# The opening of a hybrid decoder block: chunk-wise start, and conditioning rounds split evenly between DVE and PE

## The chip, the cores and the metric

One core of a Trainium2 chip runs the kernel. The metric is the device time of one execution in microseconds (us). PE is the matrix engine and PEld its weight load, DVE the vector engine, ACT the scalar engine, POOL the general one; SP only issues transfers. Each engine works through its own instructions in order and waits for others by semaphores.

## The reference

One layer of a decoder block, 512 positions, 2048 channels, all float32. What matters here is its first part; the rest (projections, a gated linear recurrence, windowed attention, branch merge, output projection, MLP) is unchanged.

```
ada = silu(c) @ w_ada + b_ada          # 2048 -> 6 x 2048
shift1, scale1, gate1, shift2, scale2, gate2 = split(ada, 6)
h = rms_norm(x, norm1_g) * (1 + scale1) + shift1
proj = h @ w_in                        # then 11 parts of proj
```

## The kernel before

Everything is kept transposed: channels lie on the 128 partitions, the 512 positions along the row. So x and h are 16 chunks of 128x512, and every weight is cut into 128x128 pieces. For accuracy each product of a weight with h is three products in fp32r (`mm3`): the weight and h are each split into a rounded part and the rest (`hi`, `lo`), and hi*hi, hi*lo and lo*hi are added up. ACT makes `hi` (L160), DVE makes `lo` (L127).

The weights arrive in raw loads of 512 KB (three buffers, tag `raw`), each of which is two items of 128x512. `step()` handles one item: `pump_loads()` issues on SP every raw load that is allowed, at most three ahead of the split that is due; `pump_splits()` splits items up to two ahead of the one at hand; `pump_loads()` is called again; then the item's products are issued. A raw load into a buffer waits until the items of the load that was in it have been split.

`startup()` makes h and drives the first eight loops. Loop j multiplies the two h chunks 2j and 2j+1 with the weights of 12 output tiles: six steps of 12 products each. Four output tiles stay in PSUM over all loops, the other eight are added up in SBUF (`sums`, tag `O`) by DVE after each loop's products. While loop j runs, the shift and scale of the next two chunks are made, the conditioning: a vector-matrix product over 16 K-tiles of `wada1`, 256 KB each, tag `O`. They are taken in four rounds of four K-tiles: in `ada_round` the first NDV K-tiles are multiplied and accumulated by DVE (`ada_step`, tile `aa`), the others by PE, four at a time in four groups of 32 columns. At the end of a round `prefetch(KT * j + 4 * r + 4 + NADA)` asks SP for the tiles up to 12 beyond the round. `ada_end` sums over the partitions on PE (columns), and `make_h` scales, shifts and splits the two chunks. `SCH` says after which of the six steps each round comes: round 0 after step 0, round 1 after step 1, rounds 2 and 3 after step 2, `ada_end` and `make_h` after step 3. With NDV = 4, round 0 is DVE's.

All bulk transfers, x, conditioning tiles and raw loads, are issued by SP in the order in which the program reaches them. Small constants are loaded by POOL at the start. Before loop 0, x is squared and summed for the norm, and the conditioning of chunks 0 and 1 is made from 16 tiles, all on PE.

Of the kernel before, what the change touches and what calls it, by code (L numbers as in the profile page):

```python
# [10 lines left out]
F32 = mybir.dt.float32  # L11
# [6 lines left out]
P = 128  # L18
# [14 lines left out]
FIRST = ("ident", "adaT")  # L33
FILL = 288
SKEW = (1, 3)
NDV = 4
SCH = ((0,), (1,), (2, 3), (4, 5), (), ())
BUFS = {"A": 32, "O": 25, "C": 16, "T": 6, "L": 5, "ada": 3, "raw": 3, "wt": 4, "B": 32, "S": 2}
WT = 7 * 2 * P
MLP = ("B", "S")  # L40
# [49 lines left out]


@with_exitstack
def tile_block(ctx, tc, xT, cT, wada1, wada2, badaT, g1T, g2T, wg0, win, wbat, wbhg, wout, wfg, wst,
               wff2, lbT, hggT, qgT, kgT, sinks, table, ident_d, mask_d, onehot_d, neg_d, outT):
    nc = tc.nc
    pl = Plan()
# [18 lines left out]
    def nm(s):  # L115
        uid[0] += 1
        return f"{s}_{uid[0]}"
# [54 lines left out]
    def take(tag, shape=None, dt=F32, name=None):  # L172
        pl.live[tag] = pl.live.get(tag, 0) + 1
        return home(tag).tile(shape or [P, T], dt, tag=tag, bufs=BUFS[tag], name=nm(name or tag))
# [12 lines left out]
    def mx():  # L187
        pl.live["mx"] = pl.live.get("mx", 0) + 1
        return psM.tile([P, T], F32, tag="mx", name=nm("mx"))
# [5 lines left out]
        return tiny.tile([P, n], F32, tag="s", bufs=8, name=nm("s"))  # L195


    def cload(name, shape, src, dt=F32):
        t = (fst if name in FIRST else cst).tile(shape, dt, name=name)
        G.dma_start(out=t, in_=src)  # L200
        return t

    c_sb = cload("c_sb", [P, KT], cT)
    x_t = []
    for kt in range(KT):
        t = take("C")
        SP.dma_start(out=t, in_=xT[:, kt, :])  # L207
        x_t.append(t)
    g1_sb = cload("g1_sb", [P, KT], g1T)
    adaT = cload("adaT", [P, 96], badaT)  # L210
    tab_sb = cload("tab_sb", [32, 16], table)
    oneh = take("T", [32, 383])
    G.dma_start(out=oneh, in_=onehot_d)
    negc = take("T", [16, 383])
    G.dma_start(out=negc, in_=neg_d)
    ident = cload("ident", [P, P], ident_d)
    qg_sb = cload("qg_sb", [P, 1], qgT)
    kg_sb = cload("kg_sb", [P, 1], kgT)
# [117 lines left out]
    raws = {}  # L336
    wts = {}

    def pump_loads():
        done = items[state["split"]][0] if state["split"] < len(items) else len(loads)  # L340
        while state["load"] < len(loads) and state["load"] < done + BUFS["raw"]:
            src, n = loads[state["load"]]
            if state["load"] in doubled and not room("S") and not room("T", 5):
                return
            raw = act.tile([P, n], F32, tag="raw", bufs=BUFS["raw"], name=nm("raw"))
            if state["load"] in doubled:
                n -= 2 * P
                raw = raw[:, 0:n]
                full, src = src, src[:, 0:n]
            SP.dma_start(out=raw, in_=src)  # L350
            if state["load"] in doubled:
                c = 2 * P
                tag = "S" if room("S") else "T"
                s = take(tag)
                SP.dma_start(out=s, in_=src[:, 0:2 * c])
                G.dma_start(out=s.rearrange("p (n c) -> p n c", c=c),  # L356
                            in_=full[:, None, 3 * c:4 * c].to_broadcast([P, 2, c]), accum_op=ALU.add)
                raw = (raw, s, tag)
            raws[state["load"]] = raw
            state["load"] += 1  # L360
# [129 lines left out]
                drop("O")  # L490

    held = {}
    for j in range(KT // 2):
        for g in range(G0 // 2):
            if g % 2 == 0:
                ld = add_load(wg0[j, g // 2], 1024)

            def emit(hi, lo, j=j, g=g):
                for s in range(2):
                    i = 2 * g + s  # L500
                    if i not in HELD:
                        ps = mx()
                    elif j == 0:
                        ps = held[i] = acc() if i in HELD[:NACC] else mx()
                    else:
                        ps = held[i]
                    stop = i not in HELD or j == KT // 2 - 1
                    for k in range(2):
                        c = slice((2 * s + k) * P, (2 * s + k + 1) * P)
                        mm3(ps, hi[:, c], lo[:, c], h[2 * j + k], (i not in HELD or j == 0) and k == 0, stop and k == 1)  # L510
                    start_evac(i, j, ps)
            add_item(ld, (g % 2) * T, T, emit)
    n_start = len(items)

# [99 lines left out]
    def xload(n):  # L614
        def pre():
            xr[n] = take("T")
            SP.dma_start(out=xr[n], in_=xT[:, n, :])
        return pre

    def out_post(n):  # L620
# [450 lines left out]
    rv = dram.tile([16, 383], F32, name="rv")  # L1071
    rap = rv[:, :]

    def bias_rows():
        psb = mx()
        mm(psb[0:16, 0:383], tab_sb, oneh)
        tt(negc, psb[0:16, 0:383], negc, ALU.add)
        drop("mx")
        G.dma_start(out=rv, in_=negc)
        drop("T", 2)  # L1080

    def startup():
        nf = [0]
        raw = {}

        def prefetch(n):
# [3 lines left out]
                SP.dma_start(out=raw[j, kt], in_=wada1[j, kt])  # L1090
                nf[0] += 1

        prefetch(NADA)
        ps = mx()
        for kt in range(KT):
            sq = take("T")
            sact(sq, x_t[kt], AF.Square)
            if kt % 2 == 0:
                sq0 = sq
            else:  # L1100
                tt(sq, sq0, sq, ALU.add)
                mm(ps, ones, sq, kt == 1, kt == KT - 1)
                drop("T", 2)
        c32 = take("L", [P, KT, 32])
        vcopy(c32, c_act[:, :, None].to_broadcast([P, KT, 32]))
        r1, w = take("T"), take("T")
        run(rstd_g(ps, 1.0 / D, r1, w))
        drop("T")
        drop("mx")
        for kt in range(2):  # L1110
            tt(x_t[kt], x_t[kt], r1, ALU.mult)
        make_lb()
        cell = {}

        def ada_round(j, r):
            nd = NDV if j else 0
            if r == 0:
                cell["ps"] = mx()
                if nd:
                    cell["a"] = ada_acc()  # L1120
            ps = cell["ps"]
            for g in range(4):
                kt = 4 * r + g
                if kt < nd:
                    ada_step(cell["a"], raw.pop((j, kt)), kt)
                else:
                    mm(ps[32 * g:32 * g + 32, :], c32[:, kt, :], raw.pop((j, kt)), 4 * r == nd, r == 3)
                drop("O")
            prefetch(KT * j + 4 * r + 4 + NADA)
            if r == 3:  # L1130
                cell["s"] = take("L")
                if nd:
                    stt(cell["s"], ps, sel, cell["a"], ALU.mult, ALU.add)
                else:
                    sact(cell["s"], ps, AF.Copy)
                drop("mx")

        def ada_end(j):
            cell["ps"] = mx()
            ada_cols(cell["s"], cell["ps"], one if NDV and j else sel)  # L1140
            drop("L")

        def make_h(j):
            c0 = 2 * j
            ps = cell["ps"]
            tt(adaT[:, 16 + c0:18 + c0], ps[:, 2:4], adaT[:, 16 + c0:18 + c0], ALU.add)
            tt(adaT[:, c0:c0 + 2], ps[:, 0:2], adaT[:, c0:c0 + 2], ALU.add)
            drop("mx")
            stt(G1[:, c0:c0 + 2], adaT[:, 16 + c0:18 + c0], 1.0, g1_sb[:, c0:c0 + 2], ALU.add, ALU.mult)
            for kt in (c0, c0 + 1):  # L1150
                t, s, b = x_t[kt], G1[:, kt:kt + 1], adaT[:, kt:kt + 1]
                hi, lo = take("A", dt=F32R), take("A", dt=F32R)
                if j == 0:
                    sact(hi, t, AF.Identity, scale=s, bias=b)
                    ts(t, t, s, ALU.mult, b, ALU.add)
                    tt(lo, t, hi.bitcast(F32), ALU.subtract)
                else:
                    stt(t, t, s, r1, ALU.mult, ALU.mult)
                    sact(hi, t, AF.Identity, bias=b)
                    stt(lo, t, b, hi.bitcast(F32), ALU.add, ALU.subtract)  # L1160
                drop("C")
                h.append((hi, lo))

        for r in range(4):
            ada_round(0, r)
            if r == 0:
                pump_loads()
            if r == 2:
                bias_rows()
        pump_splits(1)  # L1170
        ada_end(0)
        make_h(0)
        for j in range(8):
            if j == 6:
                mask_load()
            for g in range(G0 // 2):
                step(2, drive=False)
                if j < 7:
                    for r in SCH[g]:
                        if r < 4:  # L1180
                            ada_round(j + 1, r)
                        elif r == 4:
                            ada_end(j + 1)
                        else:
                            make_h(j + 1)
# [467 lines left out]
```

## Time and profile before

| | |
|---|---|
| median of 3 runs | 2715.68 us (2715.46 to 2717.07) |
| the profiled execution | 2714.99 us, its span 2713.2 us |
| busy in the span | PE 2694.4, PEld 2288.8, DVE 1681.7, ACT 1037.3, POOL 153.3 us |
| first product of a weight with h | 31.80 us after the span's start |
| loops 1 to 6 | 20.62 us each on PE |

Busy time says what an engine did, not what bounded it; that is read from the chain of work that ended last and from timelines. In a timeline row, the first number is the start and the second the time to the end of the group; a value in brackets is the idle time of that engine ahead of it, with what ended it. Rows of one engine can overlap at their ends, so times from start to start are used for sums.

### The profile page before, as it was taken

The page shows a single profiled execution, that of the slowest core. Times are in us where ns is not written, and L with a number is a line of the kernel's source. Part 1 is how long each engine was busy: PE and PEld are TensorE (multiplying, and loading weights), DVE is VectorE, ACT ScalarE, POOL GpSimd, SP SyncE. Part 2 cuts the span into 40 slices and gives each one's busy share as a digit, 9 for nine tenths or more (in the row PEclk, how much of TensorE's full clock was granted, in tenths as well). Part 3 has the DMA queues.
Part 4 walks back from the last instruction along what each step waited for, and adds up shares of the span by engine and source line. Part 5 has one row for each costly group of instructions (what it writes and reads, how often), then busy time and mean ns, then how long its engine had stood idle before and what let it go on. Part 6 is the DMA issues. An engine that isn't in the chain of part 4 may idle for free.

```text
span 2713.2 us, 38663 instructions
## 1 busy us (share of the span) xinstructions
PE 2694.4 (99%) x14742; PEld 2288.8 (84%) x14742; DVE 1681.7 (62%) x3223; ACT 1037.3 (38%) x1905; POOL 153.3 (6%) x144
## 2 busy tenths in 40 slices
PE   8999999999999999999999999999999999999999
PEld 4777777888888888888888899988999888999897
DVE  4778777655444545565387666666566655666664
ACT  4245355544222322232254334333344333433341
POOL 1000000000000000000001011110011100111110
PEclk9999999999999999999999999999999999999999
DMA  8852321344555565555334445654455544555453
GB/s 328 291 188 97 121 97 67 121 152 132 192 190 189 182 198 175 189 168 203 129 107 127 127 131 145 156 139 126 128 144 148 148 129 127 141 146 150 131 139 127
DMA packets 182649, 415.49 MB, mean 153 GB/s; under 512 B 18944, under 2 KB 48768, under 8 KB 182464
## 3 DMA queue, kind: packets, MB, share of 16 engines
q1 hardware_dynamic: 149760, 380.18, 42.9%
q0 software_dynamic: 32704, 32.85, 7.8%
q8 instruction: 116, 1.90, 0.3%
q14 instruction: 69, 0.57, 0.1%
HBM read 408.72 MB, written 4.23 MB: 152 GB/s over the span
## 4 chain that ended last, share of the span: by engine, by line
PE 98%; DVE 1%; DMA 0%; ACT 0%; issue 0%; SPq 0%; ACTq 0%
PE acc L164 70%; PE mx L164 27%; PE mx L168 1%; DMA C<-xT 0%; DVE L L131 0%; DVE wt L127 0%; DVE T L127 0%; DVE s L1267 0%; DVE C L131 0%; DVE C L138 0%; DVE s L127 0%; SPq L207 0%; ACT T L160 0%; ACT wt L160 0%; ACT L151 0%
## 5 line engine op out<-in xcount | busy, mean ns | idle before, releaser
L164 PE MATMUL acc<-A,wt 128*128 128x512 f32 (+1 forms) x5160 | 1138.0, 368 | 4.1 <-ACT A L160 1.9
L164 PEld LDWEIGHTS acc<-A,wt 128*128 128x128 f32 x5160 | 910.7, 189 | 174.1 <-issue 8.6
L160 ACT ACTIVATE wt<-raw 128x512 fp32r<-128x512 f32 (+1 forms) x820 | 528.8, 662 | 867.2 <-PE acc L164 605.2
L127 DVE TENSOR_TENSOR wt<-raw,wt 128x512 fp32r<-128x512 f32 (+1 forms) x820 | 594.8, 729 | 422.6 <-ACT wt L160 421.1
L164 PE MATMUL acc<-B,wt 128*128 128x512 f32 (+1 forms) x3540 | 734.0, 359 | 0.0
L164 PEld LDWEIGHTS acc<-B,wt 128*128 128x128 f32 x3540 | 612.3, 189 | 98.6
L164 PE MATMUL mx<-A,wt 128*128 128x256 f32 (+1 forms) x2448 | 425.5, 309 | 0.0
L164 PEld LDWEIGHTS mx<-A,wt 128*128 128x128 f32 x2448 | 359.4, 191 | 29.5 <-issue 5.0
L164 PE MATMUL mx<-B,wt 128*128 128x256 f32 (+1 forms) x1620 | 293.9, 319 | 0.0
L131 DVE SCALAR_TENSOR_TENSOR C<-acc,adaT,C 128x512 f32<-128x512 f32 x211 | 158.0, 749 | 206.4 <-PE acc L164 206.4
L164 PEld LDWEIGHTS mx<-B,wt 128*128 128x128 f32 x1620 | 247.4, 191 | 20.3
L356 POOL DMA_DIRECT2D S<-wst x87 | 104.0, 1196 | 2065.7 <-ACT B L160 1155.2
L423 DVE SCALAR_TENSOR_TENSOR ada<-ada,aa 128x512 f32<-128x512 f32 x256 | 175.3, 685 | 47.4 <-DMA ada<-wada 42.4
L164 PE MATMUL acc<-O,wt 128*128 128x512 f32 x768 | 178.6, 389 | 0.0
L164 PEld LDWEIGHTS acc<-O,wt 128*128 128x128 f32 x768 | 144.2, 188 | 29.9
L160 ACT ACTIVATE T<-T 128x256 f32<-128x256 f32 (+1 forms) x218 | 104.4, 508 | 109.4 <-DVE T L127 106.8
L160 ACT ACTIVATE wt<-T 128x512 fp32r<-128x512 f32 x145 | 87.8, 621 | 76.7 <-DVE T L127 74.5
L127 DVE TENSOR_TENSOR wt<-T,wt 128x512 fp32r<-128x512 f32 x145 | 96.8, 684 | 0.0
L127 DVE TENSOR_TENSOR T<-T,raw 128x256 f32<-128x256 f32 x145 | 61.5, 424 | 28.1 <-DMA T<-wst 24.1
L160 ACT ACTIVATE T<-acc 128x512 f32<-128x512 f32 x34 | 20.3, 597 | 152.6 <-PE acc L164 152.6
L127 DVE TENSOR_TENSOR T<-S,raw 128x256 f32<-128x256 f32 x87 | 36.7, 421 | 42.7 <-DMA S<-wst 38.6
L160 ACT ACTIVATE B<-T 128x512 fp32r<-128x512 f32 x80 | 47.3, 602 | 34.0 <-DVE T L127 19.8
(170 smaller groups left out, 1350.1 us busy)
## 6 DMA issues: line engine op xcount, KB each, us to landing
raw<-win SPq DMA_DIRECT2D x128, 512.0 KB, 4.0
ada<-wada SPq DMA_DIRECT2D x256, 256.0 KB, 4.4
raw<-wff SPq DMA_DIRECT2D x128, 512.0 KB, 3.6
raw<-wst SPq DMA_DIRECT2D x116, 384.0 KB, 3.7
O<-wada SPq DMA_DIRECT2D x128, 256.0 KB, 5.2
S<-wst SPq DMA_DIRECT2D x87, 256.0 KB, 3.9
S<-wst POOLq DMA_DIRECT2D x87, 256.0 KB, 4.3
raw<-wout SPq DMA_DIRECT2D x32, 512.0 KB, 4.0
```

What stands on the lines that cost most here:

```text
L127: nc.vector.tensor_tensor(out=out, in0=in0, in1=in1, op=op)
L131: nc.vector.scalar_tensor_tensor(out=out, in0=in0, scalar=scalar, in1=in1, op0=op0, op1=op1)
L160: nc.scalar.activation(out=out, in_=in_, func=func, **kw)
L164: PE.matmul(out, lhsT=lhsT, rhs=rhs, start=start, stop=stop)
L168: PE.transpose(out=out, in_=in_, identity=ident)
L356: G.dma_start(out=s.rearrange("p (n c) -> p n c", c=c), in_=full[:, None, 3 * c:4 * c].to_broadcast([P, 2, c]), accum_op=ALU.add)
L423: nc.vector.scalar_tensor_tensor(out=t, in0=t, scalar=1.0, in1=cb, op0=ALU.mult, op1=ALU.mult, accum_out=adaq[:, i, q:q + 1])
```

## The change

- The weights of the conditioning of chunks 0 and 1 come a second time as `wada0`, 16 tiles of 256 KB, of which the first eight hold all that chunk 0 needs and the other eight all that chunk 1 needs. `first_chunk(s)` makes one chunk from eight tiles. Chunk 0 is made before loop 0, chunk 1 within step 1 of loop 0.
- In loop 0, items 0 to 2 are first multiplied with chunk 0 alone, and with chunk 1 when it is there. Small products on constants (`keep`) run on PE between the pieces of the first chunk.
- SP's order at the start: 16 tiles of x, six of `wada0`, a raw load, two of `wada0`, a raw load, eight of `wada0`, a raw load, eight tiles of the next pair. x lies in memory as 16 contiguous blocks.
- Ten small loads move from POOL at the start to SP ahead of loop 1; the bias product (`bias_rows`) and `make_lb` move from the opening to the start of loop 2. Four of the 16 squares of x go to DVE.
- NDV becomes 8: rounds 0 and 1 are DVE's. `ada_rounds` is a generator that stops after the third and the sixth K-tile, so DVE's eight K-tiles come as three after step 0, three after step 1 and two after step 2, where rounds 2 and 3 on PE follow. In loop 0 (`SCH0`) six come after step 2, the others with rounds 2 and 3 after step 3, and `ada_end` and `make_h` after step 4.
- `make_h` makes both scaled chunks and both rounded parts before the two rests.

```diff
-NDV = 4
-SCH = ((0,), (1,), (2, 3), (4, 5), (), ())
+NDV = 8
+SCH0 = ((), (), (0, 1), (2,), (4, 5), ())
+SCH = ((0,), (1,), (2,), (4, 5), (), ())
...
-        SP.dma_start(out=t, in_=xT[:, kt, :])
+        SP.dma_start(out=t, in_=xT[kt])
...
+            def two_products(i, k):
+                todo2 = []
+                for i, ps, w in begun[i:i + 2]:
+                    c = slice((2 * (i % 2) + k) * P, (2 * (i % 2) + k + 1) * P)
+                    mm(ps, w[0][:, c], h[k][0], k == 0, False)
+                    mm(ps, w[1][:, c], h[k][0], False, False)
+                    todo2.append((ps, w[0][:, c], i not in HELD and k == 1))
+                for ps, wc, last in todo2:
+                    mm(ps, wc, h[k][1], False, last)
...
+                if j == 0 and g < 3:
+                    for i in (2 * g, 2 * g + 1):
+                        begun.append((i, bank(i, j), (hi, lo)))
+                    two_products(2 * g, 0)
+                    if g == 1:
+                        second.pop()()
+                    if g < 2:
+                        return
+                    for i in range(0, 6, 2):
+                        two_products(i, 1)
+                        for i, ps, _ in begun[i:i + 2]:
+                            start_evac(i, j, ps)
+                    return
...
+    def load_rest():
+        for t, src in late_loads:
+            SP.dma_start(out=t, in_=src)
...
-        prefetch(NADA)
+        fetch0(KT // 2 - 2)
+        pump_loads(1)
+        fetch0(KT // 2)
+        pump_loads(2)
+        fetch0(KT)
+        pump_loads()
+        prefetch(KT + 8)
...
         def ada_round(j, r):
-            nd = NDV if j else 0
+            nd = NDV
...
                 if kt < nd:
                     ada_step(cell["a"], raw.pop((j, kt)), kt)
+                    if g == 2 and r == 0 or g == 1 and r == 1:
+                        yield
                 else:
                     mm(ps[32 * g:32 * g + 32, :], c32[:, kt, :], raw.pop((j, kt)), 4 * r == nd, r == 3)
                 drop("O")
             prefetch(KT * j + 4 * r + 4 + NADA)
...
+        def ada_rounds(j):
+            for r in range(4):
+                yield from ada_round(j, r)
...
+        def first_chunk(s):
+            x, g, b = x_t[s], G1[:, s:s + 1], adaT[:, s:s + 1]
+            if s == 0:
+                tt(x, x, r1, ALU.mult)
+                pump_splits(0)
+            ps = mx()
+            for i in range(KT // 2):
+                for u in range(2):
+                    kt, t = 2 * i + u, raw0[KT // 2 * s + i]
+                    mm(ps[32 * (kt % 4):32 * (kt % 4) + 32, 0:256], c32[:, kt, :], t[:, 256 * u:256 * u + 256], kt < 4,
+                       kt > KT - 5)
+                drop("O")
+                if s == 0 and i % 2:
+                    keep(1)
...
+            if s == 0:
+                keep(7)
...
         for j in range(8):
+            if j == 1:
+                rest = load_rest()
+            if j == 2:
+                make_lb()
+                bias_rows(*rest)
...
                 step(2, drive=False)
                 if j < 7:
-                    for r in SCH[g]:
+                    for r in (SCH if j else SCH0)[g]:
                         if r < 4:
-                            ada_round(j + 1, r)
+                            if r == 0:
+                                cell["go"] = ada_rounds(j + 1)
+                            next(cell["go"], None)
```

## Rows read from the trace of the kernel before

**Rows 1.** The page: chain of work that ended last, share by engine.
```profile
PE 98%; DVE 1%; DMA 0%; ACT 0%; issue 0%; SPq 0%; ACTq 0%
```

**Rows 2.** Timeline of PE, loop 1: start, us, engine, line, operation, out<-in, count.
```profile
55.22 1.52 PE L164 MATMUL acc<-A,wt 128*128 128x512 f32 x6
...
57.94 1.52 PE L164 MATMUL acc<-A,wt 128*128 128x512 f32 x6
...
63.25 1.52 PE L164 MATMUL mx<-A,wt 128*128 128x512 f32 x6
64.70 1.92 PE L164 MATMUL mx<-O,L 128*32 128x512 f32 x16
66.56 3.06 PE L164 MATMUL mx<-A,wt 128*128 128x512 f32 x12
...
75.84 0.39 PE L164 MATMUL acc<-A,wt 128*128 128x512 f32 x1
```

**Rows 3.** Timeline of SP's issues, 39 to 66 us, two of them singly.
```profile
39.38 0.33 SPq L350 DMA_DIRECT2D raw<-wg  x1
...
56.20 0.33 SPq L350 DMA_DIRECT2D raw<-wg  x1
56.62 1.81 SPq L1090 DMA_DIRECT2D O<-wada  x4
58.05 0.38 SPq L1090 DMA_DIRECT2D O<-wada  x1
62.22 0.33 SPq L350 DMA_DIRECT2D raw<-wg  x1
...
64.78 0.43 SPq L1090 DMA_DIRECT2D O<-wada  x1
```

**Rows 4.** DMA issues at 0.74, 39.38, 58.05, 64.78: KB, us from issue to landing.
```profile
C<-xT SPq DMA_DIRECT2D x1, 256.0 KB, 2.7
raw<-wg SPq DMA_DIRECT2D x1, 512.0 KB, 5.1
O<-wada SPq DMA_DIRECT2D x1, 256.0 KB, 4.5
O<-wada SPq DMA_DIRECT2D x1, 256.0 KB, 4.9
```

**Rows 5.** Timeline of DVE in loop 1, 58 to 62 us.
```profile
58.14 0.69 DVE L127 TENSOR_TENSOR O<-mx,O 128x512 f32<-128x512 f32 x1 [0.48 <-PE mx L164]
58.75 0.48 DVE L136 TENSOR_SCALAR aa<-O,c_act 128x512 f32<-128x512 f32 x1
59.27 2.33 DVE L131 SCALAR_TENSOR_TENSOR aa<-O,c_act,aa 128x512 f32<-128x512 f32 x3
61.51 0.68 DVE L127 TENSOR_TENSOR wt<-raw,wt 128x512 fp32r<-128x512 f32 x1
```

**Rows 6.** Timeline of PE and its weight load, 25 to 32 us.
```profile
25.51 0.81 PE L164 MATMUL mx<-T,tab_sb 32*16 32x383 f32 x2
26.25 1.91 PE L164 MATMUL mx<-O,L 128*32 128x512 f32 x8
27.11 0.14 PEld L164 LDWEIGHTS mx<-O,L 128*32 128x32 f32 x2 [0.49 <-DMA O<-wada]
31.80 0.49 PE L164 MATMUL acc<-A,wt 128*128 128x512 f32 x1 [1.91 <-ACT A L160]
```

**Rows 7.** The chain's first pieces: start, us, what; the second is x's 14th tile.
```profile
0.74 0.39 SPq L207
...
8.92 6.60 DMA C<-xT
```

**Rows 8.** One loop: stretch, length, busy us (count) by engine, PEclk, DMA share, GB/s.
```profile
104.65:125.27 20.62, 20.62 (x105) 14.82 (x105) 15.34 (x27) 4.90 (x8) 0.00 (x0) 1.00 0.80 280
```

**Rows 9.** The same columns for two stretches of the opening.
```profile
20.00:30.00 10.00, 9.21 (x38) 2.63 (x34) 5.38 (x16) 3.19 (x7) 0.51 (x1) 1.00 1.04 411
30.00:40.00 10.00, 7.38 (x24) 5.57 (x24) 7.24 (x15) 3.16 (x5) 0.00 (x0) 0.83 1.05 408
```

More of the change, by code (lines that the diff above doesn't have):

```diff
@@ L92, in tile_block @@
 @with_exitstack
-def tile_block(ctx, tc, xT, cT, wada1, wada2, badaT, g1T, g2T, wg0, win, wbat, wbhg, wout, wfg, wst,
+def tile_block(ctx, tc, xT, cT, wada0, wada1, wada2, badaT, g1T, g2T, wg0, win, wbat, wbhg, wout, wfg, wst,
                wff2, lbT, hggT, qgT, kgT, sinks, table, ident_d, mask_d, onehot_d, neg_d, outT):
@@ L195, in small, with cload @@
         return tiny.tile([P, n], F32, tag="s", bufs=8, name=nm("s"))
-    def cload(name, shape, src, dt=F32):
-        t = (fst if name in FIRST else cst).tile(shape, dt, name=name)
-        G.dma_start(out=t, in_=src)
+    late_loads = []
+    def cload(name, shape, src, now=False):
+        t = (fst if name in FIRST else cst).tile(shape, F32, name=name)
+        if now:
+            G.dma_start(out=t, in_=src)
+        else:
+            late_loads.append((t, src))
         return t
-    c_sb = cload("c_sb", [P, KT], cT)
+    c_sb = cload("c_sb", [P, KT], cT, True)
     x_t = []
@@ L206, in tile_block @@
         t = take("C")
-        SP.dma_start(out=t, in_=xT[:, kt, :])
+        SP.dma_start(out=t, in_=xT[kt])
         x_t.append(t)
-    g1_sb = cload("g1_sb", [P, KT], g1T)
-    adaT = cload("adaT", [P, 96], badaT)
+    g1_sb = cload("g1_sb", [P, KT], g1T, True)
+    adaT = cload("adaT", [P, 96], badaT, True)
     tab_sb = cload("tab_sb", [32, 16], table)
[L212 to L215, printed above, removed]
     ident = cload("ident", [P, P], ident_d)
@@ L337, in tile_block, with pump_loads @@
     wts = {}
-    def pump_loads():
+    def pump_loads(n=BUFS["raw"]):
         done = items[state["split"]][0] if state["split"] < len(items) else len(loads)
-        while state["load"] < len(loads) and state["load"] < done + BUFS["raw"]:
-            src, n = loads[state["load"]]
+        while state["load"] < len(loads) and state["load"] < done + n:
+            src, w = loads[state["load"]]
             if state["load"] in doubled and not room("S") and not room("T", 5):
                 return
-            raw = act.tile([P, n], F32, tag="raw", bufs=BUFS["raw"], name=nm("raw"))
+            raw = act.tile([P, w], F32, tag="raw", bufs=BUFS["raw"], name=nm("raw"))
             if state["load"] in doubled:
-                n -= 2 * P
-                raw = raw[:, 0:n]
-                full, src = src, src[:, 0:n]
+                w -= 2 * P
+                raw = raw[:, 0:w]
+                full, src = src, src[:, 0:w]
             SP.dma_start(out=raw, in_=src)
@@ L492, in tile_block @@
     held = {}
+    second = []
+    begun = []
     for j in range(KT // 2):
@@ L496, in tile_block, with bank @@
                 ld = add_load(wg0[j, g // 2], 1024)
[L498 to L507, printed above, removed]
+            def bank(i, j):
+                if i not in HELD:
+                    return mx()
+                if j == 0:
+                    held[i] = acc() if i in HELD[:NACC] else mx()
+                return held[i]
@@ new lines, in one_product @@
+            def one_product(ps, w, i, j, k):
+                c = slice((2 * (i % 2) + k) * P, (2 * (i % 2) + k + 1) * P)
+                mm3(ps, w[0][:, c], w[1][:, c], h[2 * j + k], (i not in HELD or j == 0) and k == 0,
+                    (i not in HELD or j == KT // 2 - 1) and k == 1)
+            def two_products(i, k):
+                todo2 = []
+                for i, ps, w in begun[i:i + 2]:
+                    c = slice((2 * (i % 2) + k) * P, (2 * (i % 2) + k + 1) * P)
+                    mm(ps, w[0][:, c], h[k][0], k == 0, False)
[3 more added lines that the diff above has]
+                    mm(ps, wc, h[k][1], False, last)
@@ new lines, in emit @@
+            def emit(hi, lo, j=j, g=g, bank=bank, one_product=one_product, two_products=two_products):
+                if j == 0 and g < 3:
[11 more added lines that the diff above has]
+                    return
+                for i in (2 * g, 2 * g + 1):
+                    ps = bank(i, j)
@@ L508, in emit @@
                     for k in range(2):
-                        c = slice((2 * s + k) * P, (2 * s + k + 1) * P)
-                        mm3(ps, hi[:, c], lo[:, c], h[2 * j + k], (i not in HELD or j == 0) and k == 0, stop and k == 1)
+                        one_product(ps, (hi, lo), i, j, k)
                     start_evac(i, j, ps)
+            if j == 0 and g in (1, 2):
+                ahead_of[len(items)] = 3 - g
             add_item(ld, (g % 2) * T, T, emit)
@@ L616, in pre @@
             xr[n] = take("T")
-            SP.dma_start(out=xr[n], in_=xT[:, n, :])
+            SP.dma_start(out=xr[n], in_=xT[n])
         return pre
@@ L1072, in tile_block, with bias_rows @@
     rap = rv[:, :]
-    def bias_rows():
+    def load_rest():
+        for t, src in late_loads:
+            SP.dma_start(out=t, in_=src)
+        oneh, negc = take("T", [32, 383]), take("T", [16, 383])
+        SP.dma_start(out=oneh, in_=onehot_d)
+        SP.dma_start(out=negc, in_=neg_d)
+        return oneh, negc
+    def bias_rows(oneh, negc):
         psb = mx()
@@ L1082, in startup @@
     def startup():
-        nf = [0]
+        nf = [KT]
         raw = {}
@@ L1091, in prefetch, with fetch0 @@
                 nf[0] += 1
-        prefetch(NADA)
+        def fetch0(n):
+            while nf0[0] < min(n, KT):
+                i = nf0[0]
+                raw0.append(take("O"))
+                SP.dma_start(out=raw0[i], in_=wada0[i])
+                nf0[0] += 1
+        nf0, raw0 = [0], []
+        fetch0(KT // 2 - 2)
[5 more added lines that the diff above has]
+        prefetch(KT + 8)
         ps = mx()
         for kt in range(KT):
-            sq = take("T")
-            sact(sq, x_t[kt], AF.Square)
+            sq = take("A")
+            if kt % 4 == 1:
+                tt(sq, x_t[kt], x_t[kt], ALU.mult)
+            else:
+                sact(sq, x_t[kt], AF.Square)
             if kt % 2 == 0:
@@ L1102, in startup @@
                 mm(ps, ones, sq, kt == 1, kt == KT - 1)
-                drop("T", 2)
+                drop("A", 2)
         c32 = take("L", [P, KT, 32])
@@ L1109, in startup @@
         drop("mx")
-        for kt in range(2):
-            tt(x_t[kt], x_t[kt], r1, ALU.mult)
-        make_lb()
         cell = {}
         def ada_round(j, r):
-            nd = NDV if j else 0
+            nd = NDV
             if r == 0:
                 cell["ps"] = mx()
-                if nd:
-                    cell["a"] = ada_acc()
+                cell["a"] = ada_acc()
             ps = cell["ps"]
@@ L1131, in ada_round @@
                 cell["s"] = take("L")
[L1132 to L1135, printed above, removed]
+                stt(cell["s"], ps, sel, cell["a"], ALU.mult, ALU.add)
                 drop("mx")
+        def ada_rounds(j):
+            for r in range(4):
+                yield from ada_round(j, r)
         def ada_end(j):
             cell["ps"] = mx()
-            ada_cols(cell["s"], cell["ps"], one if NDV and j else sel)
+            ada_cols(cell["s"], cell["ps"], one)
             drop("L")
@@ L1152, in make_h @@
                 hi, lo = take("A", dt=F32R), take("A", dt=F32R)
[L1153 to L1160, printed above, removed]
-                drop("C")
@@ L1162, in make_h @@
[L1162 to L1169, printed above, removed]
+                stt(t, t, s, r1, ALU.mult, ALU.mult)
+                sact(hi, t, AF.Identity, bias=b)
+                h.append((hi, lo))
+            for kt in (c0, c0 + 1):
+                hi, lo = h[kt]
+                stt(lo, x_t[kt], adaT[:, kt:kt + 1], hi.bitcast(F32), ALU.add, ALU.subtract)
+                drop("C")
@@ new lines, in startup, with keep @@
+        warm = mx()
+        def keep(n):
+            for _ in range(n):
+                mm(warm[:, 0:P], ones, ones)
+        def first_chunk(s):
[12 more added lines that the diff above has]
+                    keep(1)
+            t = take("L")
+            sact(t[:, 0:256], ps[:, 0:256], AF.Copy)
+            drop("mx")
+            cs = mx()
+            for j in range(2):
+                mm(cs[:, j:j + 1], t[:, j * P:(j + 1) * P], sel)
+            drop("L")
+            if s == 0:
+                keep(7)
+            else:
+                drop("mx")
+            tt(adaT[:, 16 + s:17 + s], cs[:, 1:2], adaT[:, 16 + s:17 + s], ALU.add)
+            tt(adaT[:, s:s + 1], cs[:, 0:1], adaT[:, s:s + 1], ALU.add)
+            drop("mx")
+            stt(G1[:, s:s + 1], adaT[:, 16 + s:17 + s], 1.0, g1_sb[:, s:s + 1], ALU.add, ALU.mult)
+            hi, lo = take("A", dt=F32R), take("A", dt=F32R)
+            sact(hi, x, AF.Identity, scale=g, bias=b)
+            ts(x, x, g, ALU.mult, b, ALU.add)
+            tt(lo, x, hi.bitcast(F32), ALU.subtract)
+            drop("C")
+            h.append((hi, lo))
@@ L1170, in startup @@
+        first_chunk(0)
         pump_splits(1)
-        ada_end(0)
-        make_h(0)
+        tt(x_t[1], x_t[1], r1, ALU.mult)
+        second.append(lambda: first_chunk(1))
         for j in range(8):
+            if j == 1:
[3 more added lines that the diff above has]
+                bias_rows(*rest)
             if j == 6:
@@ L1591 @@
     a1 = cc(w_ada[:, 0:4096].reshape(KT, P, 2, 8, 256).transpose(3, 0, 1, 2, 4).reshape(8, KT, P, 512))
+    a0 = cc(w_ada[:, 0:4096].reshape(8, 2, P, 2, KT, P)[:, :, :, :, :2].transpose(4, 0, 2, 1, 3, 5).reshape(KT, P, 512))
     a2 = cc(w_ada[:, 4096:].reshape(KT, 4, 32, 4, 16, P).transpose(3, 1, 4, 5, 2, 0).reshape(256, P, T))
@@ L1629 @@
     arrays = {
-        "xT": cc(I["x"][0].T.reshape(KT, P, T).transpose(1, 0, 2)),
+        "xT": cc(I["x"][0].T.reshape(KT, P, T)),
         "cT": chans(I["c"][0]),
-        "wada1": a1, "wada2": a2,
+        "wada0": a0, "wada1": a1, "wada2": a2,
         "badaT": chans(I["b_ada"][0]),
```

## The prediction

> **What bounds the kernel now.** I read the chain that ended last first: TensorE (PE) carries 98% of the span [rows 1], so an edit counts only where it takes PE work away, lets PE start earlier, or makes PE wait. Then the timeline of one opening loop, engine by engine. A loop takes 75.84 - 55.22 = 20.62 us on PE without a gap [rows 2]. Twelve 128x512 products take 57.94 - 55.22 = 2.72 us; the six loop steps are 72 products, 16.3 us. The rest is conditioning: one round (four K-tiles) alone after step 1, two rounds after step 2, the column products after step 3. The stretch 57.94 to 63.25 holds 18 products (4.08 us) and the round that stands alone, so that round costs 5.31 - 4.08 = 1.23 us. The two rounds together cost 66.56 - 64.70 = 1.86 us, and from their end to the next loop it is 75.84 - 66.56 = 9.28 us.
>
> In the same loop I read what SP issues [rows 3], how long each transfer takes to land [rows 4], and what DVE does between [rows 5]. Last, the opening ahead of the loops: PE's first product starts at 31.80 us, after an idle 1.91 us, the last conditioning tile having landed at 27.11 [rows 6]; until then PE follows the transfers.
>
> The profiled execution took 2714.99 us, its span 2713.2; the median of the runs is 2715.68. Sums are made on 2714.99, and 0.7 is added at the end.
>
> **Part 1: the opening.** Today chunks 0 and 1 of h need 16 conditioning tiles behind 16 tiles of x; after the change chunk 0 needs 8, the first products run on half of item 0 to 2's K range, and chunk 1's 8 tiles land behind them. But the first loop also needs the 16 tiles of the next pair, eight of which (K-tiles 8 to 15) PE multiplies after step 3. Count SP's queue in tiles of 256 KB (a raw load is two): x 16, new chunk tiles 16, raw loads 0 to 4 10, tiles 0 to 7 8, tiles 8 to 15 8. PE's rounds end on the 58th. Today the 58th is the end of the load issued at 39.38, landing 5.1 later, at 44.5 [rows 3, 4]; the 14th landed at 8.92 + 6.60 = 15.52 [rows 7]. That is 0.658 us a tile; but x itself took (15.52 - 3.44)/13 = 0.93 a tile from the first landing (issue 0.74, 2.7 later [rows 4, 7]). Ten of the 14 small POOL loads leave that stretch and x is laid out contiguously. If x came at 0.658 too, all would land 3.5 us earlier; if nothing changes, 0. I take the middle, 1.7, since four small loads stay and the rows don't say which of the two causes holds.
>
> The 58th then lands at 42.8 (41.0 to 44.5). PE ended 26.25 + 1.91 = 28.16 for the landing at 27.11 [rows 6], 1.05 later: rounds end at 43.9. Is PE there by then? x whole at about 15.1; its norm took 6.6 us behind the last x tile today, so 21.7, when the 26th tile (the last of chunk 0) lands as well; from the last tile to the first product is 31.80 - 27.11 = 4.7 us today, so the first product comes at 26.4 at the latest, 18 half products follow; chunk 1's last tile (36th) lands at 28.3, its h at 33.0 at the latest; 18 products and step 3's 12 end at 39.8. Yes: PE waits for tiles 8 to 15, not these for PE. Behind the rounds stand steps 4 and 5 and the columns, 9.28 less step 3's 2.72 = 6.56. Loop 1 starts at 50.4 instead of 55.22: **4.8 us gained** (3.1 to 6.6). The keep-warm products and chunk products lie in stretches in which PE waits for transfers.
>
> Here the Trainium skill bears on x: "DMA: Bandwidth & Descriptors", section "Latency and other measured facts", says that transfers with very large power-of-two row pitches (512 KiB up, at worst half rate at 4 MiB) run slow, and that contiguous tiles mend it; x's pitch is 32 KiB, which the page doesn't cover, and no row separates it from the small loads. By that rule, stretched to here, the gain would be 6.6 instead of 4.8.
>
> **Part 2: the bias product.** It stood at 25.51 with 0.81 us [rows 6], among waits for tiles; now it stands ahead of loop 2, where PE has no gap: +0.8. The ten small loads now go on SP ahead of loop 1's loads; SP's issues take 0.33 to 0.43 us each [rows 3], some 4.2 us, free before loop 1's second load is wanted 6 us into the loop. Nothing, or up to 1.4 if they queue.
>
> **Part 3: one round less on PE in loops 1 to 6.** Four more K-tiles go to DVE, so PE loses the round of 1.23 us. DVE is busy 15.34 us of a loop [rows 8]; four accumulations of 0.75 (59.27 to 61.51 for three [rows 5]) make 18.3 of the 19.4 that would be left: it fits, and the new order of the two scale-shift pieces takes two ACT waits out. By this alone -7.4 us.
>
> **Part 4: what moves with it on SP.** The loader asks for K-tiles 12 to 15 of the pair when round 0 is over. Today round 0 ends in step 0, so SP issues: raw load (56.20), the four tiles (56.62 to 58.43), then step 1's raw load (62.22) [rows 3]. That last one waits for the split of item 3 on DVE: the split runs 61.51 to 62.19 and the issue is at 62.22 [rows 3, 5]. After the change round 0's fourth K-tile comes behind step 1, so SP holds that raw load *ahead* of the four tiles, and all four stand behind DVE's split. DVE's order up to the split is the sum of item 0 (released by PE, 58.14), then the K-tile steps, then the split; with three K-tile steps instead of four it ends 0.75 earlier: issue at 62.22 - 0.75 = 61.47, 6.25 us into the loop. From such a raw load's issue to the landing of the fourth tile behind it: 58.05 + 4.5 - 56.20 = 6.35, and 64.78 + 4.9 - 62.22 = 7.46 [rows 3, 4]. The second is the same load in the same place, with tiles following; the first has nothing behind it. I take 6.9. Tile 15 lands 13.15 us into the loop; today 7.3, where PE wants it at about 10.4, so there was slack of 3.
>
> PE in the new loop reaches round 2 at 8.2 and would end both at 10.1; it waits in round 3 for tile 15, ends at 13.15 + 1.05 = 14.2, and everything behind it on PE (item 3, columns) is held. The loop becomes 14.2 + 9.28 = 23.5 instead of 20.62: **+2.86**, and DVE has time to spare. Bounds by the two rows: 2.3 to 3.4. Loops 1 to 6 have it (loop 0 is in part 1, loop 7 asks for nothing): +17.2 (13.9 to 20.5). This includes the round saved.
>
> Sum: -4.8 + 0.8 + 17.2 = +13.2; 2714.99 + 13.2 = 2728.2, on the scale of the median **2728.9**. Own range: -6.6 + 0.8 + 13.9 to -3.1 + 2.2 + 20.5, that is 2723.8 to 2735.3.
>
> **Rivals.** *A, the tiles come in time:* PE gets the round back in every loop: -4.8 + 0.8 - 6 x 1.23 = -11.4, 2704.3. It holds if tile 12 to 15 land by 9 us into the loop. For it: DVE and the transfers (share 0.80 [rows 8]) have room. Against it: SP's issue times against DVE's split [rows 3, 5]. It would take an order of SP other than I read, so 0.15.
>
> *B, the wait also lowers the clock:* PE idles from the end of round 2 until tile 12 comes, 1 to 2 us, and then works tile by tile. After the idle stretch before the first product the granted clock averaged 0.83 over 30 to 40 us, the lower level being 1.2 GHz [rows 9], a loss of 1.7 us; six times that is +10: 2739. Against it: from 20 to 30 us PE worked tile by tile and the clock stayed at 1.00 [rows 9]. 0.07. The Trainium skill, "TensorE: Matmul & The Clock Gate", section "Part 1: The HAM clock gate", has the reduced clock as the default state from which activity releases the engine; by that rule this rival, 2739; the rows at 20 to 30 us speak against it here.
>
> *C, a shorter wait:* if the four tiles land some 5 us behind the raw load's issue rather than 6.4 to 7.5, the wait just eats the round and the opening's gain; the turn to a gain is at +0.7 us a loop, a wait of 1.9. Then about 2713 to 2720. 0.08.
>
> **How the numbers follow.** Forecast 0.70, A 0.15, C 0.08, B 0.07. The range takes in the forecast's own range, C and the near side of B and leaves out A: 2712 to 2738. About 0.2% (5.4 us) is what a measurement of this kernel can tell from no change. Faster 0.16 (A, the edge of C), same 0.10 (most of C, the low tail of the forecast), slower 0.74.
>
> **What would show it.** The first f32r product should start at 24 to 27 us, and loop 1 near 50. Loops 1 to 6 should take 23 to 24 us each on PE, with a wait of PE or its weight load for the conditioning tiles in the second round behind step 2; SP's four-tile issues should follow the raw load at about 6.3 us into the loop. If loops take 19.4 with tile 15 landed before round 3, part 4 is wrong, and A holds. If loop 1 starts at 52 or later, part 1's transfer count is wrong; if the clock falls in the loops, B.

## The result and the profile after

The changed kernel takes 2736.06 us (median of four runs, 2734.25 to 2736.82) against 2715.89 for the kernel before: ratio 1.0071, 95% interval 1.0059 to 1.0083. It is 20.2 us slower; forecast were 13.2. The median lies in the stated range of 2712 to 2738, but 0.8 us above 2735.3, the upper end of the forecast's own sum. The profiled span grew from 2713.2 to 2734.2.

The chain that ended last now has 2% of transfers and 2% of DVE in it, where PE had nearly all [rows 1]:

```profile
PE 94%; DMA 2%; DVE 2%; issue 0%; ACT 0%; SPq 0%; POOLq 0%; ACTq 0%
```

The timeline of PE (start, us, operation, out<-in, count, idle time ahead and what ended it) shows the opening: the first product comes at 24.60 instead of 31.80 [rows 6], the rounds that wait for the 58th tile are over at 43.6, and loop 1 starts at 50.17 instead of 55.22 [rows 2].

```profile
24.60 0.71 PE L165 MATMUL acc<-A,wt 128*128 128x512 f32 x2
...
39.61 4.09 PE L165 MATMUL mx<-O,L 128*32 128x512 f32 x16
43.63 3.04 PE L165 MATMUL mx<-A,wt 128*128 128x512 f32 x12
...
50.17 1.54 PE L165 MATMUL acc<-A,wt 128*128 128x512 f32 x6
```

Then the gain is lost. The starts of loops 2 to 7 on PE:

```profile
75.20 1.66 PE L165 MATMUL acc<-A,wt 128*128 128x512 f32 x6
...
100.23 1.52 PE L165 MATMUL acc<-A,wt 128*128 128x512 f32 x6
...
123.38 1.52 PE L165 MATMUL acc<-A,wt 128*128 128x512 f32 x6
...
146.51 1.52 PE L165 MATMUL acc<-A,wt 128*128 128x512 f32 x6
...
169.78 1.52 PE L165 MATMUL acc<-A,wt 128*128 128x512 f32 x6
...
198.15 1.52 PE L165 MATMUL acc<-A,wt 128*128 128x512 f32 x6
```

From start to start, the bias product of 0.74 us ahead of loop 2 taken out, loops 1 to 6 take 24.29, 25.03, 23.15, 23.13, 23.27 and 28.37 us; each took 20.62 in the kernel before. That is 23.5 us more in six loops. With the opening (-5.05) and the bias product (+0.74), loop 7 starts 19.2 later; 1.8 more come behind it, most of them in the MLP.

Loop 3 shows where. DVE's order up to the split, then SP, then PE:

```profile
103.15 0.69 DVE L128 TENSOR_TENSOR O<-mx,O 128x512 f32<-128x512 f32 x1 [1.38 <-PE mx L165]
103.76 0.48 DVE L137 TENSOR_SCALAR aa<-O,c_act 128x512 f32<-128x512 f32 x1
104.27 1.54 DVE L132 SCALAR_TENSOR_TENSOR aa<-O,c_act,aa 128x512 f32<-128x512 f32 x2
105.72 0.68 DVE L128 TENSOR_TENSOR wt<-raw,wt 128x512 fp32r<-128x512 f32 x1
```

```profile
106.44 0.33 SPq L352 DMA_DIRECT2D raw<-wg  x1
106.86 5.09 SPq L1132 DMA_DIRECT2D O<-wada  x10
```

```profile
108.48 1.07 PE L165 MATMUL mx<-O,L 128*32 128x512 f32 x8
110.53 3.68 PE L165 MATMUL mx<-O,L 128*32 128x512 f32 x8 [0.98 <-DMA O<-wada]
114.13 3.01 PE L165 MATMUL mx<-A,wt 128*128 128x512 f32 x12
```

The split ends at 106.40, the raw load follows at 106.44, 6.2 us into the loop, and only then the four tiles, which were issued at 1.4 us into the loop before [rows 3]. PE begins round 2 at 108.48, waits, and both rounds take 5.65 us where they took 1.86 [rows 2].

### The profile page after: what moved, and what is told of

The parts are those of the page before. It is cut to its first block, busy times and chain, and to the rows that moved or that the text cites. A ratio compares the mean times of both kernels' runs of the same rounds, so it can differ in the third digit from the quotient of the medians.

```text
span 2734.2 us, 38690 instructions
## 1 busy us (share of the span) xinstructions
PE 2706.1 (99%) x14740; PEld 2293.1 (84%) x14740; DVE 1702.9 (62%) x3258; ACT 1034.9 (38%) x1902; POOL 148.0 (5%) x134
## 4 chain that ended last, share of the span: by engine, by line
PE 94%; DMA 2%; DVE 2%; issue 0%; ACT 0%; SPq 0%; POOLq 0%; ACTq 0%
PE acc L165 68%; PE mx L165 25%; DMA O<-wada 1%; PE mx L169 1%; DMA S<-wst 1%; DVE wt L128 1%; DMA C<-xT 0%; DVE aa L132 0%; DVE T L128 0%; DVE L L132 0%; DVE s L1369 0%; SPq L213 0%; ACT wt L161 0%; DVE C L132 0%; DVE aa L137 0%
```

## The experiments

**The request moved back, DVE's share kept.** One request is added to the changed kernel:

```diff
                     ada_step(cell["a"], raw.pop((j, kt)), kt)
+                    if g == 2 and r == 0:
+                        prefetch(KT * j + 4 + NADA)
                     if g == 2 and r == 0 or g == 1 and r == 1:
                         yield
```

> The changed kernel with one line more: K-tiles 12 to 15 are requested at the end of step 0 (before the generator first stops), so SP issues them ahead of step 1's raw load again. Theory (the request's place costs PE a wait in round 3 of loops 1 to 6): the tiles land by about 7.5 us into the loop, no wait of PE for them remains, loops take 19.4 to 19.7 us instead of 23.1 to 28.4, and the whole is 2703 to 2708, faster than both kernels. Rival (DVE's eight K-tiles are too many and hold PE): loops stay at 20.6 or longer and the whole is 2711 or more.

Measured: 2709.8 us, ratio 0.9977 (0.9968 to 0.9987). In loop 3 SP issues the four tiles ahead of the raw load again, and the rounds run without a wait; the loop takes 113.27 - 93.88 = 19.39 us, and so do loops 4 to 6 (loop 2 19.54):

```profile
94.31 1.81 SPq L1132 DMA_DIRECT2D O<-wada  x4
100.08 0.33 SPq L352 DMA_DIRECT2D raw<-wg  x1
```

```profile
102.13 1.92 PE L165 MATMUL mx<-O,L 128*32 128x512 f32 x16
```

The view of busy time over that loop (the columns of [rows 8]) answers the rival: DVE is busy 17.81 of 19.39 us and PE never stops.

```profile
93.88:113.27 19.39, 19.39 (x98) 14.75 (x96) 17.81 (x31) 4.85 (x8) 0.00 (x0) 1.00 0.84 297
```

The whole came out 2 to 7 us above the forecast. Loop 1 took 23.8 us beside the bias product, since the ten small loads stand on SP ahead of its tiles (the fourth experiment shows it). In the profiled execution, which took 2711.15 us, some 3 us more were lost in the MLP (below). So the wait is the price of the place of the request, and not of DVE's share.

**The request moved, in the kernel before.** Now the kernel before gets the new place of the request and nothing else.

```diff
+            if r == 1 and j > 1:
+                prefetch(KT * j + 4 + NADA)
...
-            prefetch(KT * j + 4 * r + 4 + NADA)
+            if r or j < 2:
+                prefetch(KT * j + 4 * r + 4 + NADA)
```

> The kernel before, with the request for K-tiles 12 to 15 in loops 1 to 6 made behind step 1's raw load, nothing else. Theory: the raw load is issued at 7.0 us into the loop, the last tile lands 6.3 to 7.5 later, PE ends round 3 at 14.4 to 15.6 instead of 11.3, each of the six loops gains 3.0 to 4.2 us, the whole is 2734 to 2741. Rival (the wait came from DVE's greater share, not from the place of the request): within 2 us of the kernel before.

Measured: 2742.61 us, ratio 1.0102 (1.0085 to 1.0118). Loop 3 runs from 104.88 to 130.46; the four tiles start at 112.36, and round 3 goes tile by tile:

```profile
112.36 10.79 SPq L1090 DMA_DIRECT2D O<-wada  x16
```

```profile
114.36 1.06 PE L164 MATMUL mx<-O,L 128*32 128x512 f32 x8
116.09 1.04 PE L164 MATMUL mx<-O,L 128*32 128x512 f32 x2 [0.68 <-DMA O<-wada]
117.37 1.05 PE L164 MATMUL mx<-O,L 128*32 128x512 f32 x2 [0.23 <-DMA O<-wada]
119.55 1.72 PE L164 MATMUL mx<-O,L 128*32 128x512 f32 x4 [1.13 <-DMA O<-wada]
121.20 3.03 PE L164 MATMUL mx<-A,wt 128*128 128x512 f32 x12
```

Loops 1 to 5 take 24.0 to 25.6 us, 3.4 to 5.0 more than before. Loop 6 takes 27.9 (179.08 to 207.01), 7.3 more: there PE waits 4.16 us at once, while POOL loads four tiles of another kind (the bias bands, below). Loops 2, 3 and 6 lie above the top of what was expected, and so does the whole, by 1.6 us. Nothing but the place of one request was changed: it alone costs 26 us (2716.4 beside it).

**The opening alone.** This kernel has the changed opening and loop 0, but loops 1 to 6 have four K-tiles on DVE and the rounds where they stood.

```diff
-SCH = ((0,), (1,), (2,), (4, 5), (), ())
+SCH = ((0,), (1,), (2, 3), (4, 5), (), ())
...
-            nd = NDV
+            nd = NDV if j == 1 else 4
...
-                    if g == 2 and r == 0 or g == 1 and r == 1:
+                    if j == 1 and (g == 2 and r == 0 or g == 1 and r == 1):
...
                 yield from ada_round(j, r)
+                if j > 1:
+                    yield
```

> The changed kernel's opening and loop 0, but in loops 1 to 6 the conditioning as before: four K-tiles on DVE after step 0, round 1 on PE after step 1, rounds 2 and 3 after step 2. Theory: loop 1 starts at about 50.2, loops take 20.62, the bias product adds 0.8: 2711 to 2713. Rival (the opening shifts transfers of the later loops so that its gain is given back): 2715 or more.

Measured: 2714.69 us, ratio 0.9994 (0.9985 to 1.0003), between the two expectations and not told apart from the kernel before. Loop 1 starts at 50.11, 5.1 us earlier, and ends late: loop 2 starts at 74.64, and from there loops take 20.6 to 20.8 us. Loop 1's 23.8 us beside the bias product are 3.2 too many, as in the first experiment: SP issues the ten small loads from 51.78 to 58.1 and only then the four tiles. So the rival holds in part: the opening gains 5 us, and 3 of them go in loop 1 to what was moved out of the opening.

**The ten small loads behind loop 1's tiles.** The kernel of the first experiment, with

```diff
-            if j == 1:
-                rest = load_rest()
-            if j == 2:
+            if j == 3:
                 make_lb()
                 bias_rows(*rest)
...
                         else:
                             make_h(j + 1)
+                if j == 1 and g == 3:
+                    rest = load_rest()
```

> The kernel of e1_early (tiles 12 to 15 requested in step 0), and the ten small loads go on SP behind step 3 of loop 1 instead of ahead of the loop, with the bias product at the start of loop 3. Theory (in e1_early SP issued the ten loads ahead of loop 1's tiles, so its loop 1 took 23.8 us beside the bias product instead of 19.4): loop 1 takes 19.4 to 19.8, the whole is 2704 to 2707. Rival (loop 1 is long since the transfers are still behind from the opening): loop 1 stays above 22, the whole is 2709 to 2711.

Measured: 2705.48 us (2705.22 to 2706.86), ratio 0.9961 (0.9949 to 0.9974): the best of all kernels run here, 10.8 us under the kernel before (2716.29 beside it). Rival A, in which the tiles come in time, had added up to 11.4. Loop 1 starts at 50.73 and loop 2 at 70.18, 19.45 us later; SP's tiles go out at 52.45, the small loads from 65.61 on. Loop 2 takes 20.1 us. Loops 1 and 2 together take 0.8 more than two of the later loops, so behind the tiles the small loads cost that much at most.

```profile
50.73 1.56 PE L165 MATMUL acc<-A,wt 128*128 128x512 f32 x6
...
70.18 1.52 PE L165 MATMUL acc<-A,wt 128*128 128x512 f32 x6
```

```profile
52.45 2.91 SPq L1132 DMA_DIRECT2D O<-wada  x4
57.00 0.33 SPq L352 DMA_DIRECT2D raw<-wg  x1
57.42 7.29 SPq L1132 DMA_DIRECT2D O<-wada  x12
65.01 0.33 SPq L352 DMA_DIRECT2D raw<-wg  x1
65.61 0.34 SPq L1110 DMA_DIRECT2D tab_sb<-table  x1
```

**Loop 6 and the bias bands.** In loop 6 of the changed kernel POOL loads four bias bands of 256 KB beside the last tiles. The fourth tile took 8.1 us to land there (issued at 177.83); in loop 3 it took 4.8 (issued at 108.34). The rows give KB and us to landing, loop 3 first. PE waits 3.08 us at once in loop 6.

```profile
O<-wada SPq DMA_DIRECT2D x1, 256.0 KB, 4.8
O<-wada SPq DMA_DIRECT2D x1, 256.0 KB, 8.1
```

```profile
175.79 0.72 POOL L1428 DMA_DIRECT2D O<-rv  x1 [79.88 <-DVE aa L132]
177.63 1.54 POOL L1428 DMA_DIRECT2D O<-rv  x2 [1.12 <-DVE aa L132]
```

```profile
178.03 1.06 PE L165 MATMUL mx<-O,L 128*32 128x512 f32 x8
182.18 1.96 PE L165 MATMUL mx<-O,L 128*32 128x512 f32 x4 [3.08 <-DMA O<-wada]
184.87 2.99 PE L165 MATMUL mx<-O,L 128*32 128x512 f32 x4 [0.73 <-DMA O<-wada]
```

In the experiment SP loads these four bands, behind its raw loads and so after loop 6:

```diff
-            G.dma_start(out=t, in_=bass.AP(rap.tensor, rap.offset + 2 * i * 383, [[1, P], [383, 2], [1, 256]]))
+            (SP if c == 0 else G).dma_start(out=t, in_=bass.AP(rap.tensor, rap.offset + 2 * i * 383, [[1, P], [383, 2], [1, 256]]))
```

> The changed kernel, but the four bias bands of the first attention half are loaded by SP behind the raw loads instead of by POOL, whose loads ran beside the last four conditioning tiles in loop 6. Theory (loop 6 took 28.4 us instead of 23.2 since these loads delayed the tiles and the clock fell behind the wait): loop 6 takes 23 to 24 us, the whole is 2730 to 2733. Rival (loop 6 is long for another reason): no change, 2735 to 2737.

Measured: 2730.41 us, ratio 1.0052 (1.0037 to 1.0067). Loop 6 runs from 170.25 to 193.48, 23.23 us: the 5.1 us that it took beyond loops 3 to 5 go with the bands. Its fourth tile (issued at 178.30) lands as in loop 3 again:

```profile
O<-wada SPq DMA_DIRECT2D x1, 256.0 KB, 4.9
```

**The clock in the wait.** In the profiled execution of the changed kernel the granted clock falls to its lower level, 1.2 GHz, behind the wait in loops 2 and 6 (columns of [rows 9]):

```profile
88.00:90.00 2.00, 2.00 (x6) 0.36 (x4) 0.00 (x0) 0.00 (x0) 0.00 (x0) 0.50 1.06 405
...
186.00:188.00 2.00, 2.00 (x4) 0.34 (x4) 0.10 (x1) 0.00 (x0) 0.00 (x0) 0.50 0.00 0
```

The experiment puts four small products on constants into the wait:

```diff
+            if r == 2 and j > 1:
+                idle = mx()
+                for _ in range(4):
+                    mm(idle[:, 0:P], ones, ones)
+                drop("mx")
             prefetch(KT * j + 4 * r + 4 + NADA)
```

> The changed kernel, with four products on constants (about 0.9 us) behind round 2 in loops 1 to 6, in the stretch in which PE waits for tile 12. Theory (PE's idle stretch in the wait lets the clock fall in loops 2 and 6): the granted clock stays at 1.00 in loops 1 to 5 at least, one or both falls go, and the whole is 2 to 5 us below the changed kernel, 2731 to 2734. Rival (the clock falls for another reason, or the products hold round 3 back): no change or slower, 2735 to 2740.

Measured: 2734.42 us, ratio 1.0066 (1.0051 to 1.0082). In the profiled execution both falls are gone:

```profile
86.00:92.00 6.00, 4.47 (x15) 1.39 (x14) 2.24 (x4) 0.00 (x0) 0.00 (x0) 1.00 1.03 368
183.00:190.00 7.00, 5.92 (x18) 2.35 (x19) 1.85 (x3) 0.00 (x0) 0.30 (x1) 1.00 0.47 185
```

Loop 6 takes 26.29 instead of 28.37 and loop 2 24.66 instead of 25.03, but loops 1, 3, 4 and 5 take 0.1 to 0.4 more. The medians differ by 1.6 us, just short of what was expected, and the runs of the two kernels overlap (2733.59 to 2735.47 against 2734.25 to 2736.82).

Where the clock falls changes from run to run, so this pair says less than it seems. With the bands moved (above) it fell in loop 1 alone; in the next two kernels it fell in loops 1 and 6, and in loop 6 alone. Their loop 2 is the changed kernel's, and without any product in the wait the clock stayed at 1.00 in it and it took 23.6 to 23.9 us. The row is loop 1 with the bands moved:

```profile
62.00:64.00 2.00, 2.00 (x4) 0.33 (x4) 0.00 (x0) 0.00 (x0) 0.00 (x0) 0.50 0.96 323
```

So only loop 6 bears on the clock's price: 27.1, 27.4 and 28.4 us where it fell, 26.3 where it held. The clock's share is some 1 to 2 of the 20 us. The rule of the Trainium skill that stood with rival B ("TensorE: Matmul & The Clock Gate", "Part 1: The HAM clock gate") agrees with loop 6: with work put into the idle stretch the clock held at 1.00. On loop 2 these runs do not bear it out or speak against it.

**What made x slow to land.** Two kernels, each the changed one with one part undone, each from one profiled execution (2735.15 and 2734.42 us). In the first, x has its old layout again, where it is read the second time too:

```diff
-        SP.dma_start(out=t, in_=xT[kt])
+        SP.dma_start(out=t, in_=xT[:, kt, :])
```

> The changed kernel with x laid out as before (rows of 2 KB at a pitch of 32 KB). If the layout made x slow to land, the last sum of squares starts 1.0 to 1.8 us later than 15.69 and loop 1 at 51 to 52; if the small POOL loads made it slow, both stay within 0.3 us (15.7 and 50.2).

In the second, the ten small loads are back on POOL at the start:

```diff
-        if now:
-            G.dma_start(out=t, in_=src)
-        else:
-            late_loads.append((t, src))
+        G.dma_start(out=t, in_=src)
```

> The changed kernel with the ten small loads back on POOL at the start (x contiguous). If the small loads made x slow to land, the last sum of squares starts 1.0 to 1.8 us later than 15.69 and loop 1 at 51 to 52; if the layout did, both stay within 0.3 us. Loop 1 itself, without the small loads on SP ahead of its second raw load, should be about 1 us shorter than the 24.3 us of the changed kernel.

Measured, the last sum of squares on DVE: in the changed kernel, with x in rows, and with the small loads on POOL:

```profile
15.69 0.69 DVE L128 TENSOR_TENSOR A<-A,A 128x512 f32<-128x512 f32 x1 [0.49 <-ACT A L161]
```

```profile
15.74 0.69 DVE L128 TENSOR_TENSOR A<-A,A 128x512 f32<-128x512 f32 x1 [0.48 <-ACT A L161]
```

```profile
17.02 0.69 DVE L128 TENSOR_TENSOR A<-A,A 128x512 f32<-128x512 f32 x1
```

Loop 1 starts at 50.17, 50.08 and 52.15, the last just above the 51 to 52 that was expected; in the other kernels here with the changed opening it starts between 49.77 and 50.73. So the layout of x shows no effect, and the small loads cost 1.3 us of x's landing and about 2 us of the opening. Without them on SP loop 1 takes 23.77 us instead of 24.29, half of the 1 us expected.

## Why the prediction was right, and where its sizes were off

*Direction, mechanism, place: right.* Part 4's steps one by one: the raw load was put at 6.25 us into the loop and comes at 6.2 (106.44 - 100.23); the fourth tile was put 6.9 behind it and lands 108.34 + 4.8 - 106.44 = 6.7 behind it; the rounds were to end at 14.2 and end at 13.9; loops were to take 23.5, and loops 3 to 5 take 23.1 to 23.3. The two counter-tests, the request moved back in one kernel and moved away in the other, show the cause.

*The number: in part luck.* The time lies above the forecast's own sum and inside the stated range only because the range was widened for the near side of rival B. What filled the gap was mostly something else. Loop 6, with the bands that no term held, makes up 4.9 of the 7 us that were missing (28.37 against the forecast's 23.5); the clock, which is B's mechanism, is some 1 to 2 us of these.

*Part 1: right.* The 58th tile set the end of the rounds, 43.6 against 43.9, and loop 1 starts 5.05 us earlier against 4.8. That the 1.7 us came out well is luck: it was the middle between nothing and all, since two causes could not be told apart. The runs show only one of them at work, the small loads, and none from the layout. The rule of the Trainium skill on row pitch ("DMA: Bandwidth & Descriptors", "Latency and other measured facts") stretched to x's 32 KiB would have added 1.8; the measurement decides against stretching it.

*Parts 2 and 3: right in size.* The bias product costs 0.74 us against 0.8, and with the request back in its old place a loop takes the 1.23 us less that were put.

*The term that was mis-sized is "loops 1 to 6 have it: +17.2".* Taking one loop six times gave 17.2 where 23.5 were measured, 6.3 too little, because loops 1, 2 and 6 are not like loops 3 to 5:
- Loop 1 (+3.7 instead of 2.9). The ten small loads were put at nothing, with 1.4 as the bound if they queue. SP got to loop 1's second raw load at 57.30, 7.1 us into the loop instead of 6.2. The estimate of 4.2 us for their issues was too short: they take from 51.85 to 57.20.

```profile
51.85 0.42 SPq L1110 DMA_DIRECT2D tab_sb<-table  x1
...
57.30 0.37 SPq L352 DMA_DIRECT2D raw<-wg  x1
```

- Loop 2 (+4.4): the fourth tile took 83.39 + 5.5 - 81.55 = 7.3 from the raw load's issue to its landing, near the upper of the two bounds, and the clock fell. This is one execution: in three other kernels with the same loop 2 the clock held there and the loop took 3.0 to 3.3 more than before.
- Loop 6 (+7.8): POOL's bands were not looked for. Part 4 followed SP's queue only; the bands are in another queue, but beside them SP's fourth tile lands 3.3 us later. In the kernel before PE waited for no tile in that loop, which took 20.62 like the others.

*Rival B* was set as all six loops or none, at +10. In the profiled executions that have the wait, with nothing put into it, the clock falls in one or two loops of six, and not always in the same ones; in loop 6, where it can be priced, it cost 0.9 to 2.1 us.

*The last 1.8 us* behind loop 7 were in no term. In the MLP the time by which PE lags behind the kernel before moves by small steps, in places where the code of all these kernels is the same. In the first experiment, between 2440 and 2640 us, PE waited 2.1 us for DVE's splits; in the kernel before and in the best one it did not wait there at all. What sets it is open; it was not tried.

## What to carry to other kernels

SP issues in the order of the program, so the place of a request is part of its price: a request that is put behind one that waits for a buffer waits with it (26 us in the kernel before, for one request moved). When a generator or a new schedule splits a step, follow every request that the step issues to its new neighbours in the queue, not only the arithmetic. Look at the other queues too: POOL's bands made loop 6 the longest. Moving work between engines paid exactly what the round cost, 1.23 us a loop, as soon as the request went back to its old place. And what is moved out of a crowded opening must land somewhere with slack: ten tiny loads cost 2 us at the start, 3 to 4 ahead of loop 1's tiles, and at most 0.8 behind them.

## What the runs showed that was not expected

Ten loads of less than 0.2 MB in all, on POOL, delay 4.2 MB of x by 1.3 us, while rows of 2 KB at a pitch of 32 KB land as fast as contiguous blocks (last sum of squares at 15.74 against 15.69). Four band loads on POOL raise the time to landing of a 256 KB tile on SP from 4.8 to 8.1 us; without them it is 4.9. The granted clock fell behind waits of 1 to 4 us, but in different loops from one run to the next. And ten small loads hold SP longer than their rows add up to: nine rows of 0.41 to 0.43 us and one of 1.09 make 4.9, and the ten occupy SP for 5.35 us.
